# A two-layer trunk: weight casts and a square moved behind evacuations, and gate loads in other buffers

## The chip, the cores and the metric

The kernel runs on one core of a Trainium2 chip. The metric is the device time of one launch in microseconds (us), as a median of several runs. One execution was also taken with the hardware profiler; its trace gives the start and the length of every instruction. The engines are named as in the profile: PE (matmuls), PEld (its weight loads), DVE (vector), ACT (scalar), POOL (GpSimd) and SP, which here only sends DMAs.

## The reference

The input is 1024 tokens of 1024 channels in float32, the output has the same shape. Two layers, each `x + mixer(RMSNorm(x))`, and a last RMSNorm:

```python
def mixer_ab(h, ...):                       # layer 0
    u_s5, g_s5, q, k, v, g_ret = jnp.split(h @ w_in, cuts, axis=-1)
    y_s5 = s5_mixer(u_s5, ...) * jax.nn.silu(g_s5)      # state space, GELU, GLU
    y_ret = retention(q, k, v) * jax.nn.silu(g_ret)    # rotary positions inside
    return jnp.concatenate([y_s5, y_ret], axis=-1) @ w_out

def mixer_conv(h, ...):                     # layer 1
    a, b, g = jnp.split(h @ w_in, 3, axis=-1)
    u = a * jax.nn.sigmoid(b)
    u = causal_depthwise_conv31(u) + conv_b
    u = layernorm_over_channels(u) * ln_g + ln_b
    return (jax.nn.silu(u) * jax.nn.silu(g)) @ w_out
```

## The kernel before

**Layout.** Activations lie with the channels on the 128 partitions, in 8 blocks `nb` of 128 channels, and with the tokens in two halves `h` of 512 on the free axis. Every large product is made with three matmuls of 128x512 for one block of the contraction (`mm3`, L174 to L176): high part by high part, high weights by low activations, low weights by high activations. Operands are rounded to `fp32r`; the low part is what the rounding left out.

**Weights.** `plan` writes down the order in which weight blocks of 512 KB are used. `wnext(name, ahead=2)` hands out the next one and, if that is not yet done, emits the loads of this one and of the two behind it. A load (`wload`) is a DMA on SP into `wf` (L162), a cast on ACT to `wh` (L164), and a subtract on POOL or DVE to `wl` (L165); `wf`, `wh` and `wl` have three buffers each. Weights that are used a second time (`wload_again`) get their low part by DMA from DRAM (L150) in place of the subtract. These are `wl_woc` in the last stage.

**Order.** The program's text is not the order on the engines. A planner with its own estimates of durations orders the instructions of each engine; `with self.at(...)` sets a due time, and `with self.tc.issue_after(x)` keeps what is emitted inside it behind instruction x. In the queue of one engine everything waits behind an instruction that waits. PSUM banks of one kind are handed round: a product that needs a bank waits until the evacuation of its last user is done. `mm` banks are three; in layer 0 there are five `aux` banks beside them.

**Layer 0, values (L1023).** `ret_values_wide` makes the values of the first two pairs of heads, for each half h: four weight blocks `v0_h_j`, each a quarter of the contraction for 512 channels, four banks, one for each 128 tokens, and behind the last block four `nc.scalar.mul` on ACT (L1041) that bring the banks to SBUF scaled by `Rtok`. The next weights in `plan` are k1 and q1. After the values PE turns the keys (`ktp`, L1054), each into an `aux` bank.

**Layer 0 end, layer 1 start.** `w_out(h, nbs)` (L1280 on) makes the output product of layer 0 over 16 blocks, adds the residual on DVE (`x`, L1293), stores it, and adds its square to a running sum (`square_sum`: the square on ACT at L399, the sum on POOL at L404). `ab(h)` makes b and a of layer 1 for each block: weights `cb`, product `mm_b`, tanh on ACT (L1326) for the sigmoid, weights `ca`, product `mm_a`, and `u` on DVE (L1335). In `plan` two blocks of the second half's output product stand ahead of `ab(0)`, the other six behind it. The tanh needs another activation table than what ran before, so an ACT_TABLE_LOAD stands ahead of it.

**Layer 1, convolution.** The convolution runs in pairs of blocks: 26 of 31 taps on DVE (L1393), the first five on ACT and POOL (L1372, L1373), from `u` (tag `u`, five buffers) into a PSUM accumulator. `gates` writes `silu(g)` to DRAM (`gs_d`). `conv_norm(h)` makes the sums over channels with narrow matmuls (`cst` at L435, from `cs` and `cq`, the sums on POOL at L1444 and L1445), spreads mean and deviation over the partitions (`cR`, `cD`), and for each block: norm, SiLU, load of the gate `gl` (L1480), product with it (L1481), and the split into `zh` and `zl` (L1157). In the second half blocks 3, 5 and 7 run on POOL, the others on DVE. `w_out_c` makes the last product `mm_oc` and the final sums (`s2q`, L1507 and L1510).

**Slots in layer 1.** The pool `lp` has rings by tag: `tp` three buffers (partial taps on ACT and POOL, later also the second half's gates), `u` five (the conv's inputs), `ev` three, `ld` two. A load into a ring waits until the last reader of that buffer is done.

Of the kernel before, what the change touches and what calls it, by code (L numbers as in the profile page):

```python
# [11 lines left out]
F32 = mybir.dt.float32  # L12
F32R = mybir.dt.float32r
I32 = mybir.dt.int32
AF = mybir.ActivationFunctionType
# [4 lines left out]
P = 128  # L20
# [3 lines left out]
HALF = 512  # L24
# [27 lines left out]
class Trunk:  # L52
# [59 lines left out]
    def wnext(self, name, ahead=2):  # L112

        assert self.wseq[self.wgot][1] == name, (self.wseq[self.wgot][1], name)
        for i in range(self.wgot, min(self.wgot + ahead + 1, len(self.wseq))):
            if i not in self.wissued:
                self.wissued[i] = self.wload(*self.wseq[i])
        self.wgot += 1
        return self.wissued.pop(self.wgot - 1)

    def wload(self, src, name):

# [900 lines left out]
    def ret_values_wide(self):  # L1023

        nc = self.nc
        res = []
        for h in range(2):
            vt = self.rp.tile([P, 4, HALF], F32, name=f"v_0_{h}", tag="v", bufs=2)
            pss = [self.bank(f"mm_v0_{h}_{b}") for b in range(4)]
            for j in range(4):  # L1030
                wh, wl = (t[:].rearrange("p (k a) n -> p k (a n)", a=4) for t in self.wnext(f"v0_{h}_{j}"))
                for b in range(4):
                    o = slice(b * P, (b + 1) * P)
                    for k in range(2):
                        kb = 2 * j + k
                        xh, xl = self.xs[h][kb]
                        nc.tensor.matmul(pss[b][:], xh[:, o], wh[:, k, :], start=kb == 0, stop=False)
                        nc.tensor.matmul(pss[b][:], xh[:, o], wl[:, k, :], start=False, stop=False)
                        nc.tensor.matmul(pss[b][:], xl[:, o], wh[:, k, :], start=False, stop=kb == KB - 1)
            for b in range(4):  # L1040
                nc.scalar.mul(vt[:, b, :], pss[b][:], self.Rtok[:, 4 * h + b:4 * h + b + 1])  # L1041
            res.append(vt)
        return lambda p, b, hh: res[b // 4][:, b % 4, (2 * p + hh) * P:(2 * p + hh + 1) * P]

    def ret_heads(self, pair, K, Q, qadds, mask, kdec, V, turned):
# [113 lines left out]
    def layer0_back_and_layer1(self, st):  # L1159
        nc, A = self.nc, self.A  # L1160
        v, gp = nc.vector, nc.gpsimd
        lp = self.lp
# [73 lines left out]
        for m in range(2):  # L1236
            pss = [self.bank(f"mm_glu1{2 * m + a}", aux=False) for a in range(2)]
# [11 lines left out]
        for i, x in ((6, t2), (7, t3), (4, t4)):  # L1249
            for m in range(2):  # L1250
                w = wn()
                for a in range(2):
                    n = 2 * m + a
# [9 lines left out]
        for m in range(2):  # L1263
            pss = [self.bank(f"mm_glu5{2 * m + a}", aux=False) for a in range(2)]
            for i, x in ((5, t1), (3, b22)):
                w = wn()
                for a in range(2):
                    n = 2 * m + a
# [12 lines left out]
        accs = {}  # L1281

        def w_out(h, nbs):
            for nb in nbs:
                xt = lp.tile([P, HALF], F32, name=f"xr{nb}_{h}", tag="ld", bufs=2)
                nc.sync.dma_start(xt[:], A["xT"][nb, :, hs(h)])
                ws = self.wnext(f"wos{nb}_{h}")
                wr = self.wnext(f"wor{nb}_{h}")
                ps = self.bank(f"mm_wo{nb}_{h}", aux=False)
                seq = [(ws, ys[h], kb) for kb in range(KB)] + [(wr, yr[h], kb) for kb in range(KB)]  # L1290
                self.gemm_seq(ps[:], seq, self.hold if h and nb == 0 else None)
                t = lp.tile([P, HALF], F32, name=f"x1_{nb}_{h}", tag="ev", bufs=3)
                v.tensor_tensor(t[:], ps[:], xt[:], op=ALU.add)  # L1293
                nc.sync.dma_start(self.x1_d[rows(nb), hs(h)], t[:])
                self.square_sum(lp, t, nb, h, "s1", accs)

        def h1(h):

# [21 lines left out]
        def ab(h):  # L1320
            for nb in range(8):
                wb = self.wnext(f"cb{nb}_{h}")
                pb = self.bank(f"mm_b{nb}_{h}", aux=False)
                self.gemm(pb[:], wb, hx[h])
                sg = lp.tile([P, HALF], F32, name=f"sb{nb}_{h}", tag="ev", bufs=3)
                nc.scalar.activation(sg[:], pb[:], AF.Tanh, scale=0.5)  # L1326
                wa = self.wnext(f"ca{nb}_{h}")
                pa = self.bank(f"mm_a{nb}_{h}", aux=False)
                self.gemm(pa[:], wa, hx[h])
                u = lp.tile([P, PADW + HALF], F32, name=f"u{nb}_{h}", tag="u", bufs=5)  # L1330
                if h == 0:
                    gp.memset(u[:, :PADW], 0.0)
                else:
                    nc.scalar.copy(u[:, :PADW], tail[:, nb, :])
                v.scalar_tensor_tensor(u[:, PADW:], sg[:], 1.0, pa[:], op0=ALU.add, op1=ALU.mult)  # L1335
                if h == 0:
                    nc.scalar.copy(tail[:, nb, :], u[:, HALF:])
                ub[h][nb] = u
# [70 lines left out]
        def csquare(h, nb):  # L1409
            sq = (self.opA.tile([P, HALF], F32, name=f"cvq{nb}_{h}", tag="A1") if h else  # L1410
                  lp.tile([P, HALF], F32, name=f"cvq{nb}_{h}", tag="sq", bufs=1))
            nc.scalar.activation(sq[:], cv[h][nb][:], AF.Square)
            return sq
# [24 lines left out]
        def conv_norm(h):  # L1438
            sm, acc = accs[("cv", h)]
            st = ps_cv.tile([P, HALF], F32, name=f"cst_{h}", tag="cn")  # L1440
            q7 = csquare(h, 7)
            s1, s2 = st[:, 0:256], st[:, 256:512]
            if h == 0:
                gp.tensor_tensor(sm[:], sm[:], cv[h][7][:], op=ALU.add)  # L1444
                gp.tensor_tensor(acc[:], acc[:], q7[:], op=ALU.add)  # L1445
                self.token_sums([(s1, sm[:]), (s2, acc[:])])
            else:
                self.token_sums([(s1, sm[:]), (s2, acc[:]), (s1, cv[h][7][:]), (s2, q7[:])])
            st4 = st[:].rearrange("p (k b x) -> p k b x", k=2, x=64)

            t4 = [lp.tile([P, 4], F32, name=f"cn4_{i}_{h}", tag=f"cn4_{i}", bufs=1) for i in range(4)]
            d4, q4, v4, r4 = (t[:] for t in t4)
            nc.scalar.activation(q4, st4[:, 0, :, 0], AF.Square, scale=1.0 / D)
            nc.scalar.mul(d4, st4[:, 0, :, 0], 1.0 / D)
            v.scalar_tensor_tensor(v4, st4[:, 1, :, 0], 1.0 / D, q4, op0=ALU.mult, op1=ALU.subtract)
            self.rsqrt(r4, v4)
            v.tensor_tensor(d4, d4, r4, op=ALU.mult)
            Rp = ps_cv.tile([P, HALF], F32, name=f"cR_{h}", tag="cn")
            self.spread(Rp[:], r4, lp, f"cR_{h}")
            Dp = ps_cv.tile([P, HALF], F32, name=f"cD_{h}", tag="cn")  # L1460
            self.spread(Dp[:], d4, lp, f"cD_{h}", *(("tp", 3) if h else ("dg", 1)))
            self.norm_mm[h] = self.last_stat, self.last_spread
            R = lp.tile([P, HALF], F32, name=f"RL_{h}", tag="cq", bufs=1)
            dl = lp.tile([P, HALF], F32, name=f"dl_{h}", tag="cs", bufs=1)
            for nb in range(8):
                c = cv[h][nb]

                e1, e = (v, gp) if h == 0 else (gp, gp) if nb in (3, 5, 7) else (v, v)
                z = ps_cv.tile([P, HALF], F32, name=f"zz{nb}_{h}", tag="cv") if e is v else c
                e1.tensor_tensor(z[:], c[:], (R if e1 is gp else Rp)[:], op=ALU.mult)  # L1470
                if nb == 0:
                    nc.scalar.copy(R[:], Rp[:])
                    nc.scalar.copy(dl[:], Dp[:])
                e.tensor_tensor(z[:], z[:], dl[:], op=ALU.subtract)
                nc.scalar.activation(z[:], z[:], AF.Silu, scale=self.vec(V_LNG, nb), bias=self.vec(V_LNB, nb))
                g = lp.tile([P, HALF], F32, name=f"gl{nb}_{h}", **({"tag": "tp", "bufs": 3} if h else
                                                                   {"tag": "ld", "bufs": 2}))

                with self.tc.issue_after(self.low_load["ca1"].ins) if h == 0 and nb < 2 else nullcontext():
                    nc.sync.dma_start(g[:], self.gs_d[rows(nb), hs(h)])  # L1480
                e.tensor_tensor(z[:], g[:], z[:], op=ALU.mult)  # L1481
                pt = (self.opA, "A1") if h and nb == 7 else (opB, f"B{1 - h}")
                a, b = (self.op_tile(*pt, f"z{q}{nb}_{h}") for q in "hl")
                self.split(z[:], a, b, e)
                zs[h][nb] = (a, b)
# [70 lines left out]
        for h in range(2):  # L1556
# [32 lines left out]
            with self.at(430000):  # L1589
                among = {}  # L1590
                last = [w_out_c(h, nb, quarters, among) for nb in (5, 6, 7)]
# [118 lines left out]
```

## Time and profile before

| what | value |
|---|---|
| runs | 1192.55, 1192.85, 1197.18 us; median 1192.85 us |
| profiled execution | 1193.14 us |
| its span, first to last instruction | 1191.4 us |
| granted TensorE clock | 0.999 |
| chain that ended last, share on PE | 91% |
| DMA | 261.47 MB, mean 219 GB/s |
| largest group on DVE (taps, L1393) | 398 instructions, 273.8 us |

In a row of a timeline stand the start and the length in us, the engine, the line, the operation, its output and inputs by the program's names, and in square brackets the idle time of the engine ahead of it with what ended that. In a row of the waits stand the waiting instruction, what it waited for, the total, the count and the longest, in us. A line of several equal instructions ends in x and their number.

### The profile page before, as it was taken

To read this page: it belongs to the slowest core of one execution; us is meant where nothing else is said; L and a number is where in the kernel's file an instruction comes from. 1 tells how busy PE (TensorE), PEld (TensorE's weight loads), DVE (VectorE), ACT (ScalarE), POOL (GpSimd) and SP (SyncE) were. 2 spreads that over 40 slices of the span, in tenths; PEclk is the share of its full clock that TensorE was granted. 3 is DMA by queue.
4 is the path that set the end of the run, shared out by engine and by line. 5 is a ranking of instruction groups with operands and counts; after the bars stand their busy time and mean duration, and the time that the engine had idled before them with its cause. 6 is when DMAs were issued, how large, how long until landed. Compare 5 with 4: busy or idle time off the path is not lost.

```text
span 1191.4 us, 17385 instructions
## 1 busy us (share of the span) xinstructions
PE 1178.9 (99%) x6376; PEld 987.0 (83%) x6376; DVE 847.7 (71%) x1452; ACT 483.8 (41%) x708; POOL 655.4 (55%) x448
## 2 busy tenths in 40 slices
PE   9999999999999999999999999999999999999997
PEld 7788888888888889999878888788888888888877
DVE  7975798777427459576769423599999899999533
ACT  6322233222232232233546323445445675434663
POOL 2059999988145354233563111678553577758643
PEclk9999999999999999999999999999999999999999
DMA  9344355565388676779988986656668654357774
GB/s 352 96 139 136 116 161 181 176 181 172 109 279 289 218 241 185 254 226 360 377 304 293 337 273 212 229 191 212 225 224 282 214 198 145 121 168 242 238 261 161
DMA packets 117638, 261.47 MB, mean 219 GB/s; under 512 B 10672, under 2 KB 42288, under 8 KB 116912
## 3 DMA queue, kind: packets, MB, share of 16 engines
q1 hardware_dynamic: 117552, 260.36, 65.0%
q8 instruction: 50, 0.82, 0.3%
q14 instruction: 36, 0.29, 0.1%
HBM read 181.48 MB, written 74.65 MB: 215 GB/s over the span
## 4 chain that ended last, share of the span: by engine, by line
PE 91%; DVE 3%; DMA 2%; ACT 2%; issue 1%; POOL 1%; SPq 0%; DVEq 0%; POOLq 0%; ACTq 0%
PE mm_g L174 8%; PE mm_g L176 7%; PE mm_g L175 7%; PE mm_wo L174 5%; PE mm_wo L176 5%; PE mm_wo L175 5%; PE mm_b L174 2%; PE mm_b L175 2%; PE mm_b L176 2%; PE mm_a L176 2%; PE mm_a L175 2%; PE mm_a L174 2%; PE mm_oc L175 2%; PE mm_oc L176 2%; PE mm_oc L174 2%; PE mm_u L175 2%
## 5 line engine op out<-in xcount | busy, mean ns | idle before, releaser
L1393 DVE SCALAR_TENSOR_TENSOR cv<-u,convw,cv 128x512 f32<-128x512 f32 x398 | 273.8, 750 | 12.0 <-ACT cv L1379 9.7
L1373 POOL TENSOR_TENSOR tp<-tp,tp 128x512 f32<-128x512 f32 x64 | 83.0, 1297 | 43.9 <-ACT tp L1372 42.6
L174 PE MATMUL mm_g<-xh,wh_g 128*128 128x512 f32 x256 | 101.9, 398 | 0.0
L176 PE MATMUL mm_g<-xh,wl_g 128*128 128x512 f32 x256 | 100.2, 392 | 0.0
L175 PE MATMUL mm_g<-xl,wh_g 128*128 128x512 f32 x256 | 100.2, 391 | 0.0
L1372 ACT ACTIVATE tp<-u,convw 128x512 f32<-128x512 f32 x64 | 45.5, 719 | 35.6 <-POOL tp L1373 35.3
L174 PEld LDWEIGHTS mm_g<-xh,wh_g 128*128 128x128 f32 x256 | 48.1, 188 | 11.7 <-issue 1.2
L404 POOL TENSOR_TENSOR s1q<-s1q,s1q 128x512 f32<-128x512 f32 x12 | 17.8, 1480 | 71.0 <-ACT s1q L399 71.0
L176 PEld LDWEIGHTS mm_g<-xh,wl_g 128*128 128x128 f32 x256 | 48.1, 188 | 10.3
L175 PEld LDWEIGHTS mm_g<-xl,wh_g 128*128 128x128 f32 x256 | 48.1, 188 | 9.9 <-issue 0.4
L175 PE MATMUL mm_oc<-zl,wh_woc 128*128 128x512 f32 (+1 forms) x152 | 54.5, 360 | 0.5 <-POOL zl L1157 0.5
L176 PE MATMUL mm_oc<-zh,wl_woc 128*128 128x512 f32 (+1 forms) x152 | 54.3, 359 | 0.7 <-DMA wl_woc<-lo_woc 0.7
L174 PE MATMUL mm_oc<-zh,wh_woc 128*128 128x512 f32 (+1 forms) x152 | 54.2, 362 | 0.0
L360 DVE TENSOR_TENSOR gt<-mm_g,R 128x512 f32<-128x512 f32 x32 | 21.9, 683 | 43.6 <-PE mm_g L176 43.6
L165 POOL TENSOR_TENSOR wl_v<-wf_v,wh_v 128x1024 fp32r<-128x1024 f32 x12 | 31.2, 2606 | 37.2 <-ACT wh_v L164 37.2
L174 PE MATMUL mm_b<-h1h,wh_cb 128*128 128x512 f32 x128 | 50.0, 390 | 0.9 <-DVE x L1293 0.9
L165 POOL TENSOR_TENSOR wl_glu<-wf_glu,wh_glu 128x1024 fp32r<-128x1024 f32 x14 | 34.8, 2494 | 28.7 <-ACT wh_glu L164 21.6
L174 PE MATMUL mm_g<-h1h,wh_cg 128*128 128x512 f32 x128 | 50.5, 394 | 0.0
L175 PE MATMUL mm_b<-h1l,wh_cb 128*128 128x512 f32 x128 | 50.4, 393 | 0.0
L174 PE MATMUL mm_a<-h1h,wh_ca 128*128 128x512 f32 x128 | 50.3, 393 | 0.0
L174 PE MATMUL mm_wo<-ysh,wh_wos 128*128 128x512 f32 x128 | 50.0, 390 | 0.0
L176 PE MATMUL mm_g<-h1h,wl_cg 128*128 128x512 f32 x128 | 49.9, 390 | 0.0
(490 smaller groups left out, 3665.2 us busy)
## 6 DMA issues: line engine op xcount, KB each, us to landing
wf_g<-w_ab SPq DMA_DIRECT2D x16, 512.0 KB
wf_wos<-w_out SPq DMA_DIRECT2D x16, 512.0 KB
wf_wor<-w_out SPq DMA_DIRECT2D x16, 512.0 KB
wf_cb<-w_c SPq DMA_DIRECT2D x16, 512.0 KB
wf_ca<-w_c SPq DMA_DIRECT2D x16, 512.0 KB
wf_woc<-w_out_c SPq DMA_DIRECT2D x16, 512.0 KB
wf_v<-w_v SPq DMA_DIRECT2D x12, 512.0 KB
wf_cg<-w_c SPq DMA_DIRECT2D x11, 512.0 KB
```

The costliest lines, as they stand in the source:

```text
L165: lo[i].tensor_tensor(wl[:].rearrange(fl)[:, c], wf[:, c], h.bitcast(F32), op=ALU.subtract)
L174: nc.tensor.matmul(ps, wh[:, kb, :], xh, start=start, stop=False, **more)
L175: nc.tensor.matmul(ps, wh[:, kb, :], xl, start=False, stop=False, **more)
L176: self.last_mm = nc.tensor.matmul(ps, wl[:, kb, :], xh, start=False, stop=stop, **more)
L360: nc.vector.tensor_tensor(gt[:, c], ps[:], self.R[:, c], op=ALU.mult)
L404: nc.gpsimd.tensor_tensor(a, a, sq[:], op=ALU.add)
L1372: nc.scalar.mul(sk[:], u[:, k:k + HALF], cw[:, nb, k:k + 1])
L1373: gp.tensor_tensor(s0[:], s0[:], sk[:], op=ALU.add)
L1393: v.scalar_tensor_tensor(dst[:], *tap, accs_[i][:], op0=ALU.mult, op1=ALU.add)
```

## The change

Three places are changed.

1. At the last block of the values `wnext` emits the loads of one weight block ahead instead of two, and the load of the second one ahead (q1: its DMA, cast and subtract) is emitted behind the last of the four evacuations, by a new function `wahead`.
2. The square of `x1` of block 1, second half, is put off (`self.later`), and is emitted, together with the weights that `wnext("ca0_0")` loads ahead, behind the first tanh of layer 1.
3. In `conv_norm` the second half's gates `gl` of blocks 3 to 7 take the tag `u` (the conv inputs' five buffers); those of blocks 0 to 2 stay in `tp`.

```diff
+    def wahead(self, n):
+
+        for i in range(self.wgot, self.wgot + n):
+            if i not in self.wissued:
+                self.wissued[i] = self.wload(*self.wseq[i])
...
             for j in range(4):
-                wh, wl = (t[:].rearrange("p (k a) n -> p k (a n)", a=4) for t in self.wnext(f"v0_{h}_{j}"))
+                wh, wl = (t[:].rearrange("p (k a) n -> p k (a n)", a=4)
+                          for t in self.wnext(f"v0_{h}_{j}", 1 if h and j == 3 else 2))
...
             for b in range(4):
-                nc.scalar.mul(vt[:, b, :], pss[b][:], self.Rtok[:, 4 * h + b:4 * h + b + 1])
+                last = nc.scalar.mul(vt[:, b, :], pss[b][:], self.Rtok[:, 4 * h + b:4 * h + b + 1])
             res.append(vt)
+
+        with self.tc.issue_after(last.ins):
+            self.wahead(2)
...
-                self.square_sum(lp, t, nb, h, "s1", accs)
+                if (nb, h) == (1, 1):
+                    self.later = lambda t=t: self.square_sum(lp, t, 1, 1, "s1", accs)
+                else:
+                    self.square_sum(lp, t, nb, h, "s1", accs)
...
-                nc.scalar.activation(sg[:], pb[:], AF.Tanh, scale=0.5)
-                wa = self.wnext(f"ca{nb}_{h}")
+                tanh = nc.scalar.activation(sg[:], pb[:], AF.Tanh, scale=0.5)
+
+                with self.tc.issue_after(tanh.ins) if h == 0 and nb == 0 else nullcontext():
+                    wa = self.wnext(f"ca{nb}_{h}")
+                    if (nb, h) == (0, 0):
+                        self.later()
...
-                g = lp.tile([P, HALF], F32, name=f"gl{nb}_{h}", **({"tag": "tp", "bufs": 3} if h else
-                                                                   {"tag": "ld", "bufs": 2}))
+                tag, bufs = ("ld", 2) if h == 0 else ("tp", 3) if nb < 3 else ("u", 5)
+                g = lp.tile([P, HALF], F32, name=f"gl{nb}_{h}", tag=tag, bufs=bufs)
```

## Prediction

> **What bounds the kernel now.** I read the page's busy times first, then the waits of TensorE, then the timeline of each engine around the places that the change touches, and last the two listings of the instruction order side by side.
>
> ```profile
> PE 1178.9 (99%) x6376; PEld 987.0 (83%) x6376; DVE 847.7 (71%) x1452; ACT 483.8 (41%) x708; POOL 655.4 (55%) x448
> ```
>
> TensorE (PE) is busy for 1178.9 of the 1191.4 us of the span. No edit here adds or removes a matmul, so all that can be won is in the 12.5 us in which PE stands still, and all that can be lost is new standing still. What ends those pauses is in the waits of PE:
>
> ```profile
> PE mm_b L174 <- DVE x L1293: 0.9, 1, 0.9
> PE ktp L1054 <- ACT v L1041: 0.8, 1, 0.8
> PE mm_glu L174 <- DVE gu L1260: 0.8, 1, 0.8
> PE mm_oc L176 <- DMA wl_woc<-lo_woc: 0.7, 2, 0.4
> PE rf_ps L435 <- ACT s2q L1507: 0.6, 1, 0.6
> PE mm_oc L175 <- POOL zl L1157: 0.5, 1, 0.5
> ```
>
> The columns are total us, times, longest us. Three places of this list are those that the change works on: the first row (start of layer 1's input products), the second (behind the values), and the fourth with the sixth (the last output product). The third row, `gu`, is not touched, but lies downstream of the second and comes back among the rivals.
>
> **Part 1: q's cast behind the values.** ACT and PE around 397 us:
>
> ```profile
> 396.32 1.05 ACT L164 CAST wh_q<-wf_q 128x1024 fp32r<-128x1024 f32 x1 [3.25 <-PE mm_v L1038]
> 397.27 1.26 ACT L1041 ACTIVATE v<-mm_v,Rtok 128x512 f32<-128x512 f32 x2
> ```
> ```profile
> 396.74 0.48 PE L174 MATMUL mm_k<-xh,wh_k 128*128 128x512 f32 x1
> 398.00 0.33 PE L1054 MATMUL ktp<-ident,krot 128*128 128x128 f32 x1 [0.79 <-ACT v L1041]
> ```
>
> PE goes from the values to k's product and the turned keys (`ktp`). The second `ktp` needs a bank that a `v` evacuation empties. ACT's order has the cast of `wh_q` ahead of the four `v`, and that cast cannot start before PE has let go of an older weight buffer (mm_v at L1038). So the cast holds the evacuations from 396.32 to 397.3. The `ktp` starts 1.26 us after the matmul ahead of it, where the pace is 0.23 us; 1.03 us is lost. In the new order the four `v` stand ahead of `wh_q`. The first needs only its own bank, which is complete 18 matmuls (4.1 us) before the last value matmul, and ACT stood idle for 3.25 us before the cast; so that bank is empty by 394 and the wait goes, 1.03 us.
>
> What is moved: one cast on ACT (1.05 us) and the subtract on GpSimd that makes `wl_q`. The DMA of `wf_q` keeps its place on SP (only the table `kdec` changes places with it). Behind the new place, `wh_q` starts after the last `v`, about 397.2 instead of 396.32. Its user, q's product, stands behind k's product of 48 matmuls, 48 x 0.23 = 11 us, so the 0.9 us of delay has cover; without that cover it would cost 0.9.
>
> Is the 1.03 us kept to the end? The next wait of PE is 200 us later:
>
> ```profile
> 595.60 2.87 DVE L1157 TENSOR_TENSOR y22l<-y22f,y22h 128x512 fp32r<-128x512 f32 x1
> 598.40 0.67 DVE L1260 TENSOR_TENSOR gu<-gu,mm_glu 128x512 f32<-128x512 f32 x1
> 599.00 0.68 DVE L1157 TENSOR_TENSOR y22l<-y22f,y22h 128x512 fp32r<-128x512 f32 x1
> ```
> ```profile
> 595.10 2.83 POOL L165 TENSOR_TENSOR wl_glu<-wf_glu,wh_glu 128x1024 fp32r<-128x1024 f32 x1
> ```
>
> PE waits 0.8 us for `gu`. DVE reaches `gu` at 598.40, behind a `y22l` that took 2.87 us beside GpSimd's weight subtract, where the one after it took 0.68 us alone. If those two come earlier with everything else, the gain passes; if they are held by transfers, PE arrives earlier and waits for the same `gu`. Ends 0 and 1.03; nothing in the rows decides between them, so I take the middle, **0.5**. The Trainium skill ("SBUF — State Buffer", "Who interferes with whom") says that a DVE instruction with two inputs in SBUF contends with a GpSimd instruction that reads SBUF, and that the one that holds the shared ports keeps them for its whole instruction. The 2.87 beside the 0.68 us agrees; by that rule `gu` follows GpSimd's clock and not PE's, the term would be 0, and the sum below 1.9 instead of 2.4.
>
> **Part 2: layer 1's first tanh.** ACT and PE around 759 us:
>
> ```profile
> 754.04 1.05 ACT L164 CAST wh_cb<-wf_cb 128x1024 fp32r<-128x1024 f32 x1 [6.10 <-PE mm_b L175]
> 758.80 1.05 ACT L164 CAST wh_ca<-wf_ca 128x1024 fp32r<-128x1024 f32 x1 [3.71 <-PE mm_a L175]
> 759.75 1.04 ACT L164 CAST wh_cb<-wf_cb 128x1024 fp32r<-128x1024 f32 x1
> 760.70 0.63 ACT L399 ACTIVATE s1q<-x 128x512 f32<-128x512 f32 x1
> 761.35 1.28 ACT L1326 ACT_TABLE_LOAD   x1
> 762.64 0.60 ACT L1326 ACTIVATE sb<-mm_b 128x512 f32<-128x512 f32 x1
> ```
> ```profile
> 759.01 0.39 PE L176 MATMUL mm_wo<-yr1h,wl_wor 128*128 128x512 f32 x1
> 760.27 0.47 PE L174 MATMUL mm_b<-h1h,wh_cb 128*128 128x512 f32 x1 [0.87 <-DVE x L1293]
> ```
>
> The first tanh's input is complete at about 754 (the cast at 754.04 is released by that product's matmuls), yet the tanh runs at 762.64, because two casts that wait for PE and the square of the last `x` stand ahead of it. Its bank is therefore not free when PE comes to the second `mm_b`, and PE takes the bank that `x` empties at 760.1: 1.26 us between starts instead of 0.23, 1.03 lost. In the new order ACT does `wh_cb`, table load, tanh, then `wh_ca`, `wh_cb`, square. The tanh would end at 754.04 + 1.05 + 1.28 + 0.60 = 757.0, and in the listing the second `mm_b` now waits for ACT's tanh alone. PE reaches it at 759.01 + 0.23 = 759.24, 2.2 us after that. The wait goes: **1.0**; if something still held the tanh for more than 2.2 us, part of it would stay.
>
> What is moved, with its DMA: `ca`'s load on SP keeps its order against the neighbours; its cast waits for PE's `mm_a` until 758.80 anyway and by then the tanh is over, so it costs nothing. The square (0.63) keeps its place behind the two casts; without the table load ahead of them it ends at about the same 761.3, and the running sum on GpSimd behind it is wanted only by the norm of the second half, tens of us later. The first conv input `u` comes some 3 us earlier on DVE, since it waited for the tanh. DVE goes on to the taps in a changed order; that is Part 4.
>
> **Part 3: gates of the last product.** PE, SP and GpSimd in the last stage:
>
> ```profile
> 1131.82 0.39 PE L174 MATMUL mm_oc<-zh,wh_woc 128*128 128x512 f32 x1
> ...
> 1137.96 0.50 PE L176 MATMUL mm_oc<-zh,wl_woc 128*128 128x512 f32 x1 [0.39 <-DMA wl_woc<-lo_woc]
> ...
> 1140.55 0.50 PE L175 MATMUL mm_oc<-zl,wh_woc 128*128 128x512 f32 x1 [0.48 <-POOL zl L1157]
> ```
> ```profile
> 1126.41 0.99 SPq L1480 DMA_DIRECT2D gl<-gs_d  x2
> 1127.49 0.38 SPq L150 DMA_DIRECT2D wl_woc<-lo_woc  x1
> ...
> 1132.08 0.32 SPq L1480 DMA_DIRECT2D gl<-gs_d  x1
> 1132.49 0.38 SPq L150 DMA_DIRECT2D wl_woc<-lo_woc  x1
> ```
> ```profile
> 1136.73 1.29 POOL L1481 TENSOR_TENSOR co<-gl,co 128x512 f32<-128x512 f32 x1 [2.71 <-DMA gl<-gs_d]
> 1137.97 1.29 POOL L1510 TENSOR_TENSOR s2q<-s2q,s2q 128x512 f32<-128x512 f32 x1
> 1139.22 2.52 POOL L1157 TENSOR_TENSOR zl<-co,zh 128x512 fp32r<-128x512 f32 x2
> ```
>
> From 1131.82 to 1140.55 the program has 30 matmuls; at 0.227 us they take 6.81 of the 8.73 us, so 1.92 us is lost: to two loads of `wl_woc`, to `zl`, and to slower restarts behind each. The five gates `gl` of the blocks 3 to 7 get slots that the taps free far earlier, so SP can send them between 1033 and 1106 us and not in the queue here. Two things follow. SP's `wl_woc` of block 1 goes about 0.9 us earlier (without the pair of `gl` ahead of it), that of block 2 about 0.4. The first wait (0.7 - 0.39 = 0.3) goes. The second (0.39) only shrinks: its load was used 1137.96 - 1132.49 = 5.4 us after it was sent, and is sent 0.4 earlier. And GpSimd's multiply at 1136.73, which waited 2.71 us for a `gl`, runs ahead; its three multiplies come first, then `s2q`, then `zl`, so that `zl` of block 3 ends about 1139.1 where the first of the pair ended at 1140.5. Lower end: the first wait with its restart, 0.4. Upper end 1.92. PE is then at block 3 by 1138.6, so about 0.5 of the wait for `zl` and some of the second load may stay; I take **1.1**. New on SP: a `gl` now waits in its queue for DVE's last tap at five places. The rows queued behind each are sent later than the tap's end in the old trace, so nothing is held; if a conv came late, the load behind the `gl` would be held as long.
>
> **Part 4: what is reshuffled.** Between 760 and 965 the taps of DVE, GpSimd and ACT stand in another order, and the sums of the first half's norm stand about 2 us earlier in PE's order.
>
> ```profile
> 942.26 1.28 POOL L1445 TENSOR_TENSOR cq<-cq,cvq 128x512 f32<-128x512 f32 x1
> ```
> ```profile
> 945.20 0.39 PE L175 MATMUL mm_b<-h1l,wh_cb 128*128 128x512 f32 x1
> ```
>
> The sums over `cq` now come behind the matmul of 945.20 and four narrow ones (0.45 us): 945.9, less the 1.5 us that PE is ahead by then, 944.4. GpSimd has `cq` at 943.54. That leaves 0.85 us; bounds for a new wait are 0 and 1.5 (nothing moved up on GpSimd and one more add ahead of it). With 0.85 in hand it is nearer to the first: **-0.2**.
>
> **Sum.** 0.5 + 1.0 + 1.1 - 0.2 = 2.4 us off the profiled execution of 1193.14: 1190.7. The median of the runs (1192.85) is 0.29 below that execution, so 1190.4. A measurement can tell about 0.5%, 6.0 us, from no change.
>
> **Rivals.**
>
> *The gain of 397 us dies at 598.* `gu` comes when GpSimd's third subtract and the loads let it. For it: GpSimd's subtract and DVE's `y22l` end within 0.5 us of each other, and the wait is already there. Against: nothing says that these do not start earlier too. 1.9 in place of 2.4: 1190.95. Chance 0.17.
>
> *The gates were hidden.* The last stage's transfers take as long as before, because the bytes are the same and `wl_woc` is what is late; only the 0.4 comes, and 397 is lost too: 1.0 + 0.4 - 0.2 = 1.2, so 1191.65. Chance 0.12.
>
> *Slower: the first half's conv comes late.* The place is the pair of sums near 944 us.
>
> ```profile
> 759.00:910.00 151.00, 150.13 (x670) 124.08 (x668) 139.59 (x208) 75.49 (x111) 103.24 (x70) 1.00 0.68 231
> ```
>
> In this stage (columns: length, busy PE, PEld, DVE, ACT, POOL, clock, DMA share, GB/s) DVE is busy 139.59 of 151 us. A delay of the taps there has only 11 us of slack to be made good, and PE now asks for the sums 2 us sooner. Each us by which `cq` ends later than 944.4 is a us of PE. It gets slower than before once that is 2.6 us; at 5 us it gives 1193.14 - 2.6 + 5 - 0.29 = 1195.2, and beyond 0.5% only from 8.6. Against it: `u` comes 3 us earlier, which pulls the taps forward. Chance 0.06, of which 0.03 is beyond 0.5%.
>
> *More than 0.5% faster.* That is 6 us; the three places hold 1.03 + 1.03 + 1.92 = 4.0 together. Chance 0.03.
>
> **Numbers.** The forecast has 0.62. Its own best end is a gain of 4.0: 1188.8, and 0.4 of scatter between executions gives the low end 1188.4. Its weak ends lie in the second and third cases, up to 1191.65; the range goes on to 1194.0 for the lighter half of the slower case. Faster by over 0.5% 0.03, slower by over 0.5% 0.03, within it 0.94.
>
> **What would show it.** In the profile after, PE's waits on `v` and on `x` at L1293 are gone; the first tanh runs near 756.4 to 757; the five `gl` leave SP between 1033 and 1106 us; `zl` ends by 1139.2 less the gain until then, and the two waits for `wl_woc` add up to under 0.4. Part 1 is half wrong if the wait for `gu` has grown from 0.8 towards 1.8. The prediction is wrong if PE's list has a new row of over 1 us, above all one for `cs` or `cq`, or if the three places stay.

## The result

The changed kernel takes 1189.27 us (median of 13 runs, 1187.82 to 1191.94) against 1193.34 us of the kernel before, run beside it (13 runs, 1190.82 to 1197.18). The medians lie 4.1 us apart. The ratio, which goes by all the runs and not by the two medians, is 0.9970, with a 95% interval of 0.9958 to 0.9982: 3.6 us faster, between 2.1 and 5.0. The forecast was 1190.4 us in 1188.4 to 1194.0.

The profiled execution, 1191.94 us, is the longest of the 13; its span of 1190.1 us is only 1.3 us shorter than before's. So the profile shows less of a gain than the times do. The page's first row and the list of PE's waits, of the changed kernel (lines there are 6 to 17 higher than before):

```profile
PE 1178.1 (99%) x6376; PEld 987.2 (83%) x6376; DVE 847.0 (71%) x1452; ACT 483.8 (41%) x708; POOL 654.4 (55%) x448
```
```profile
PE rt L1155 <- DVE mv L1142: 1.2, 1, 1.2
PE idle L272 <- DVE mhalf L217: 1.1, 1, 1.1
PE mm_glu L180 <- DVE gu L1270: 0.8, 1, 0.8
PE mm_glu L180 <- ACT sg L1239: 0.6, 1, 0.6
PE rf_ps L441 <- ACT s2q L1524: 0.6, 1, 0.6
PE mm_glu L182 <- POOL wl_glu L171: 0.3, 1, 0.3
PE ss L441 <- DVE ssum L267: 0.3, 1, 0.3
PE mm_oc L181 <- POOL zl L1167: 0.3, 1, 0.3
```

The waits for `v`, for `x` and for `wl_woc` are gone, that for `zl` has shrunk from 0.5 to 0.3. New are `rt` (1.2) and `sg` (0.6), both between 570 and 577 us, in a part of layer 0 that the change does not touch. No row names `cs` or `cq`.

Three landmarks on PE divide the run: the first `mm_wo`, the first `mm_oc`, and the first `rf_wait` just ahead of the last sums. From PE's timeline, before and after:

```profile
635.03 0.39 PE L174 MATMUL mm_wo<-ysh,wh_wos 128*128 128x512 f32 x1
...
1082.85 0.39 PE L174 MATMUL mm_oc<-zh,wh_woc 128*128 128x512 f32 x1
...
1183.11 1.11 PE L469 MATMUL rf_wait<-ones 128*128 128x128 f32 x8
```
```profile
636.36 0.39 PE L180 MATMUL mm_wo<-ysh,wh_wos 128*128 128x512 f32 x1
...
1083.08 0.39 PE L180 MATMUL mm_oc<-zh,wh_woc 128*128 128x512 f32 x1
...
1181.79 1.11 PE L475 MATMUL rf_wait<-ones 128*128 128x128 f32 x8
```

The changed kernel reaches `mm_wo` 1.33 us later than before did, needs 446.72 instead of 447.82 us from there to `mm_oc` (part 2 lies in this section), and 98.71 instead of 100.26 us from there to `rf_wait` (part 3). Parts 2 and 3 gave 1.10 and 1.55 us; the section with part 1 lost 1.33 in this execution.

The first tanh, on ACT:

```profile
755.37 1.05 ACT L170 CAST wh_cb<-wf_cb 128x1024 fp32r<-128x1024 f32 x1 [6.10 <-PE mm_b L181]
756.44 1.28 ACT L1339 ACT_TABLE_LOAD   x1
757.74 0.60 ACT L1339 ACTIVATE sb<-mm_b 128x512 f32<-128x512 f32 x1
```

It runs at once behind the cast, 2.2 us ahead of its use, and the second `mm_b` follows the last `mm_wo` in step (760.34, then 760.57). The five gates left SP at 1033.42, 1056.44, 1072.46, 1093.99 and 1106.46, as named. In the last stage, on SP, POOL and PE:

```profile
1126.81 0.32 SPq L156 DMA_DIRECT2D wl_woc<-lo_woc  x1
...
1132.25 0.32 SPq L156 DMA_DIRECT2D wl_woc<-lo_woc  x1
```
```profile
1132.89 3.83 POOL L1498 TENSOR_TENSOR co<-gl,co 128x512 f32<-128x512 f32 x3
1136.67 1.32 POOL L1527 TENSOR_TENSOR s2q<-s2q,s2q 128x512 f32<-128x512 f32 x1
1137.92 3.80 POOL L1167 TENSOR_TENSOR zl<-co,zh 128x512 fp32r<-128x512 f32 x3
```
```profile
1136.59 0.39 PE L182 MATMUL mm_oc<-zh,wl_woc 128*128 128x512 f32 x1
...
1138.17 0.84 PE L180 MATMUL mm_oc<-zh,wh_woc 128*128 128x512 f32 x3
1139.28 0.50 PE L181 MATMUL mm_oc<-zl,wh_woc 128*128 128x512 f32 x1 [0.27 <-POOL zl L1167]
```

No gate stands on SP between the two `wl_woc` any more; POOL makes the three products in one go from 1132.89 instead of waiting 2.71 us for the second. The first `zl` ends near 1139.2, which is the one short wait that is left. The matmul at 1136.59 is the first that uses the second `wl_woc`, and it does not wait.

The trace also holds the times at which a load's semaphore was counted up; the last of a load's 16 counts is its landing. The second `wl_woc` landed at 1137.92 in before, 5.43 us after it was sent, and at 1136.16 in the changed kernel, 3.91 us after. In the kernels of the experiments below it is 5.36 and 5.55 us without part 3 (part 1 alone, part 2 alone) and 3.78 to 4.20 with it (part 3 alone, parts 2 and 3, the whole change again). Sent at 1132.25 but with the old 5.43 us it would have landed at 1137.68, 1.1 us behind its use: it is the shorter time under way with the gates gone from the queue, and not the earlier sending, that took this wait away.

### The profile page after: what moved, and what is told of

Same layout as the page of the kernel before. It is cut to its first block, busy times and chain, and to the rows that moved or that the text cites. A ratio compares the mean times of both kernels' runs of the same rounds, so it can differ in the third digit from the quotient of the medians.

```text
span 1190.1 us, 17385 instructions
## 1 busy us (share of the span) xinstructions
PE 1178.1 (99%) x6376; PEld 987.2 (83%) x6376; DVE 847.0 (71%) x1452; ACT 483.8 (41%) x708; POOL 654.4 (55%) x448
## 4 chain that ended last, share of the span: by engine, by line
PE 47%; DMA 3%; DVE 2%; issue 1%; POOL 1%; ACT 1%; SPq 0%; DVEq 0%; POOLq 0%; ACTq 0%
PE mm_wo L180 5%; PE mm_wo L181 5%; PE mm_wo L182 5%; PE mm_g L180 2%; PE mm_b L182 2%; PE mm_g L182 2%; PE mm_b L181 2%; PE mm_g L181 2%; PE mm_b L180 2%; PE mm_a L180 2%; PE mm_a L181 2%; PE mm_a L182 2%; PE mm_oc L181 2%; PE mm_oc L182 2%; PE mm_oc L180 2%
## 5 line engine op out<-in xcount | busy, mean ns | idle before, releaser
L182 PE MATMUL mm_a<-h1h,wl_ca 128*128 128x512 f32 x128 | 50.2, 392 | 0.0
L182 PE MATMUL mm_b<-h1h,wl_cb 128*128 128x512 f32 x128 | 49.9, 390 | 0.0
```

The costliest lines, as they stand in the source:

```text
L182: self.last_mm = nc.tensor.matmul(ps, wl[:, kb, :], xh, start=False, stop=stop, **more)
```

## The experiments

Two theories on part 1: its gain is carried to the end, or it is swallowed between 550 and 600 us by what the DMA queue delivers. First the parts alone, with the others undone.

**Part 1 alone** (only the two edits in `ret_values_wide` and `wahead`).

> Part 1 alone (q's cast behind the values). Theory A (carried): the wait of ktp for v, 0.8 us with its restart 1.03, goes, and PE stays about 1.0 us ahead to the end: about 1.0 us less than before. Theory B (swallowed): the wait goes as well, PE is 1.0 ahead until about 560 us, and is then held by what the DMA queue delivers between 555 and 600 us (wf_glu, then the loads behind gu): the waits of PE between 560 and 601 us grow by about 1.0 us in sum and the time is that of before, within 0.3.

**Part 2 alone** (only `self.later` and the tanh's block).

> Part 2 alone (first tanh ahead of two casts and a square). Both theories: the wait of mm_b for x at 759 us (0.9, with restart 1.03) goes and nothing ahead of 759 changes: 1.0 us less than before. A rival, that the reshuffled taps cost at the norm of the first half, would show a new wait of PE for cs or cq near 944 us, and no gain.

**Part 3 alone** (only the tags of `gl`).

> Part 3 alone (five gates of the second half into the conv inputs' buffers). By the forecast 1.1 us less than before; by the profile after, where the two waits for wl_woc are gone and the wait for zl is 0.3, about 1.5 less. If the earlier loads of gl hold up SP between 1033 and 1106 us, a wait for a weight appears in that stretch and takes some of it back.

**Parts 2 and 3.** Against the changed kernel:

```diff
-                          for t in self.wnext(f"v0_{h}_{j}", 1 if h and j == 3 else 2))
+                          for t in self.wnext(f"v0_{h}_{j}"))
...
-        with self.tc.issue_after(last.ins):
-            self.wahead(2)
```

> The change without part 1. Theory A (carried): 1.0 us more than the whole change, about 2.5 less than before. Theory B (swallowed): the same time as the whole change within 0.3 us; PE keeps its 0.8 us wait for v at 397 us, and its waits between 560 and 601 us are smaller than in the whole change by about that.

Measured on one chip, against 1193.54 us of before (32 runs):

| kernel | median us | ratio to before, 95% |
|---|---|---|
| part 1 alone | 1193.39 | 1.0003 (0.9993 to 1.0014) |
| part 2 alone | 1191.93 | 0.9984 (0.9972 to 0.9997) |
| part 3 alone | 1191.88 | 0.9988 (0.9977 to 0.9999) |
| parts 2 and 3 | 1190.07 | 0.9973 (0.9959 to 0.9987) |

Parts 2 and 3 together have the gain of the whole change (0.9973 against 0.9970), though their interval has room for 1 us more or less. Part 1 alone has none that can be told; a gain of 1.0 us would be a ratio of 0.9992, just outside its interval. In the times that looks like the swallowed theory. The profiles tell another story. The one of part 1 alone has no wait of PE between 397 and 632 us at all, and its execution took 1190.74 us, the shortest of its 12. And of the kernels without part 1, those with part 2 alone and with parts 2 and 3 have no wait for `v` either. ACT at 395 us, of part 3 alone (with its wait of PE), of part 2 alone, and of part 1 alone:

```profile
396.49 1.05 ACT L170 CAST wh_q<-wf_q 128x1024 fp32r<-128x1024 f32 x1 [3.25 <-PE mm_v L1044]
397.44 2.42 ACT L1047 ACTIVATE v<-mm_v,Rtok 128x512 f32<-128x512 f32 x4
```
```profile
PE ktp L1060 <- ACT v L1047: 0.8, 1, 0.8
```
```profile
394.92 1.05 ACT L170 CAST wh_q<-wf_q 128x1024 fp32r<-128x1024 f32 x1 [3.29 <-DMA wf_q<-w_ab]
395.87 2.42 ACT L1047 ACTIVATE v<-mm_v,Rtok 128x512 f32<-128x512 f32 x4
```
```profile
392.88 0.68 ACT L1048 ACTIVATE v<-mm_v,Rtok 128x512 f32<-128x512 f32 x1
...
397.18 1.04 ACT L170 CAST wh_q<-wf_q 128x1024 fp32r<-128x1024 f32 x1
```

Without part 1 the evacuations follow the cast of `wh_q`, and that follows the landing of `wf_q`. The profile names `mm_v` as what ended the wait in before and in part 3 alone, but the semaphore of the load says otherwise: its last count comes at 396.22 in before and at 396.39 in part 3 alone, and 0.10 us later the cast begins, as it does in the three profiles that name the load. In five profiles with before's order on ACT (before, the relief below, and the three kernels without part 1 here) the cast began 0.07 us (before) and 0.01 us (part 3 alone) ahead of the first `ktp`, with a wait of 0.8 each; and 1.28, 2.60 and 3.12 us ahead of it in the other three, with none. Two of five: part 1 takes away about 1 us in some executions and nothing in the others, an estimate of 0.4 us on the average, from these five profiles alone. The DMA share from 380 to 396 us is 0.97 to 1.08 in windows of 5 or 6 us, with the wait and without; what makes the load land sooner or later was not found.

What becomes of that 1 us can be followed for 150 us. From the first `ktp` after the values to the first `mm_glu` PE takes 151.48 us in before and 151.53 in part 3 alone, the two with the wait, and 150.52 in part 1 alone, 150.47 in part 2 alone and in parts 2 and 3, 150.47 and 150.74 in the two profiles of the whole change. So where the wait is, it costs 1.0 us, and this is still missing when the glu starts. From the first `mm_glu` to the first `mm_wo` it then takes 85.78 us in part 1 alone, 86.92 and 89.50 in the whole change, and 86.24 to 87.18 in before and the three kernels without part 1. This scatter hides 1 us; whether it is swallowed there stays open.

**Relief of the queue at 550 us.** The second question was whether the stretch up to `mm_wo`, in which executions differ most, is set by the DMA queue. The relief sends two groups of loads later.

```diff
-                        t3 = load_sum("yt3", 1, 1, 1)
+                        with self.tc.issue_after(self.wf_load["glu4"].ins):
+                            t3 = load_sum("yt3", 1, 1, 1)
...
-                nc.sync.dma_start(xt[:], A["xT"][nb, :, hs(h)])
+                with self.tc.issue_after(self.wf_load["glu13"].ins) if h == 0 and nb < 2 else nullcontext():
+                    nc.sync.dma_start(xt[:], A["xT"][nb, :, hs(h)])
```

(`wf_load` holds the DMA of each weight.) On before:

> Before, with two groups of loads taken out of the way of the weights in the stretch 550 to 600 us: the second operand sum yt3 (8 loads of 256 KB) is sent behind the fifth weight of the glu, and the first two residual blocks xr (2 loads of 256 KB) behind its last weight. Nothing else is moved. If what PE waits for between 560 and 601 us is set by the DMA queue (swallowed), the stretch from the first mm_glu to the first mm_wo gets shorter than the 87.2 us of before, towards the 85.8 us that it took in the profile of part 1 alone where it had no waits, and the time falls by 0.5 to 1.5 us. If the DMA queue has no part in it, nothing changes.

With part 1:

> The relief with part 1. Swallowed by the DMA queue: with the queue relieved the 1.0 us of part 1 is now kept, 1.0 us less than the relief alone. If part 1 gives nothing for another reason (its wait is replaced by another one that the queue has no part in): the same as the relief alone.

With all three parts:

> The relief with all three parts. Swallowed by the DMA queue: 1.0 to 2.0 us less than the whole change, 5 to 6 us less than before, and no wait of PE over 0.5 us between 560 and 601. Otherwise: the time of the whole change.

And the whole change beside them:

> The whole change once more, on the chip of the three runs beside it, for a second profile and for their comparison: 3 to 4 us less than before. If the 2.2 us of waits for mv and sg at 570 to 576 us in its first profile belong to the change, they are there again; if they belong to that one execution, the stretch from the first mm_glu to the first mm_wo takes less than the 89.5 us of then.

Against 1193.89 us of before (35 runs): the relief 1194.26 (1.0010, 1.0001 to 1.0018), with part 1 1193.18 (1.0004, 0.9992 to 1.0015), with all parts 1191.57 (0.9987, 0.9975 to 0.9999), the whole change 1190.26 (0.9970, 0.9959 to 0.9981). The relief alone made things worse by 1.2 us (0.1 to 2.1) where a gain was expected. With all parts it lies 2.0 us above the whole change by the ratios, and with part 1 0.7 us below the relief alone; in both the intervals overlap. What it holds back was not found in its single profiles. In the one on before the stretch from the first `mm_glu` to the first `mm_wo` took 85.98 us, short as expected, but the late load below took 85.86 without any relief. It does not tell the theories of part 1 apart. The whole change came out at 0.9970 again, and its second profile has neither `rt` nor `sg`: these belong to that first execution. There ACT stood in front of a late weight of the glu, with the `rs` of the norm behind it in its queue, which PE's `rt` needs; in the second profile the same cast began at 563.34 and `rs` at 565.69, 1.4 us earlier:

```profile
564.78 1.05 ACT L170 CAST wh_glu<-wf_glu 128x1024 fp32r<-128x1024 f32 x1 [3.21 <-DMA wf_glu<-w_glu]
565.85 1.28 ACT L450 ACT_TABLE_LOAD   x1
567.14 0.30 ACT L450 ACTIVATE rs<-mv,epst 128x4 f32<-128x4 f32 x1
```

**A late load of q's weights,** without and with part 1:

```diff
-            nc.sync.dma_start(wf[:, c], src.rearrange(fl)[:, c])
+            for _ in range(2 if name == "q1" else 1):
+                nc.sync.dma_start(wf[:, c], src.rearrange(fl)[:, c])
```

> Before, with the load of q1's weights sent twice, one behind the other into the same buffer, so that it is complete some 3 to 4 us later than the 393.9 to 396.5 us at which its cast began in the profiles so far. If the wait for v at 397 us is a wait for that load (ACT holds the evacuations behind q1's cast), it is now there for certain and grows to 2.5 to 4.5 us, and the time rises by 2 to 4 us over before. If the wait has another cause, it stays at 0 to 0.8 us and the time with it.

> The same late load together with part 1. If part 1 does nothing but take the evacuations out of that load's reach, PE has no wait for v, the late weights are still in time for q's product some 10 us later, and the time is that of before within 0.5 us: 2 to 4 us less than the late load without part 1. If the late load comes through at q's product instead, a wait for wh_q or wl_q of 1 us or more appears after 405 us.

Against 1194.24 us of before (34 runs): 1192.62 (0.9986, 0.9974 to 0.9998) and 1193.30 (0.9987, 0.9975 to 0.9999). The expected 2 to 4 us of loss did not come. ACT without part 1:

```profile
392.93 0.69 ACT L1042 ACTIVATE v<-mm_v,Rtok 128x512 f32<-128x512 f32 x1 [0.56 <-PE mm_v L1040]
394.29 0.69 ACT L1042 ACTIVATE v<-mm_v,Rtok 128x512 f32<-128x512 f32 x1 [0.67 <-PE mm_v L1040]
400.76 1.05 ACT L165 CAST wh_q<-wf_q 128x1024 fp32r<-128x1024 f32 x1 [5.78 <-DMA wf_q<-w_ab]
401.71 0.68 ACT L1042 ACTIVATE v<-mm_v,Rtok 128x512 f32<-128x512 f32 x1
```

Two of the four evacuations stand ahead of the cast here: the planner, which orders by its own estimates, had moved them on its own. The cast then begins at 400.8, 3.9 us behind the first `ktp`, and PE has no wait for `v`: the two banks that are free by then are enough here. So a larger wait could not be made, but the run shows the same thing from the other side: with the first `v` ahead of the cast, a landing of `wf_q` at 400.4 to 400.7 does not reach PE, with part 1 or without. Why both are some 1.6 us faster than before by their ratios, while part 1 alone was not, stays open.

**The fourth `gu` ahead of the splits,** on the whole change:

```diff
-                        v.tensor_tensor((u2 if i == 6 else u3)[n][:], u2[n][:], ps[:], op=ALU.add)
+                        gu = v.tensor_tensor((u2 if i == 6 else u3)[n][:], u2[n][:], ps[:], op=ALU.add)
...
-                t1, b22 = load_sum("yt1", 0, 1, 0), load_split(B(1, 1), "y22", 1, False)
+                t1, b22 = load_sum("yt1", 0, 1, 0), load_split(B(1, 1), "y22", 1, False, gu)
```

> The whole change, and in the glu DVE makes the fourth gu ahead of the splits y22l instead of behind two of them; this is the gu for which PE waited 0.5 to 1.0 us near 598 us in most profiles. If that wait is DVE's order (y22l slow beside GpSimd), it goes and the time falls by about 0.8 us below the whole change, to about 0.9963 of before. If PE is held there by the loads anyway, it waits for the next thing (wl_glu or a second operand) and the time is that of the whole change.

1189.39 us, 0.9965 of before (0.9953 to 0.9976). DVE in the whole change's second profile, with PE's wait, then in this kernel, and in part 1 alone:

```profile
594.68 3.91 DVE L1167 TENSOR_TENSOR y22l<-y22f,y22h 128x512 fp32r<-128x512 f32 x2
598.52 0.68 DVE L1270 TENSOR_TENSOR gu<-gu,mm_glu 128x512 f32<-128x512 f32 x1
```
```profile
599.25 0.50 PE L180 MATMUL mm_glu<-yt3h,wh_glu 128*128 128x512 f32 x1 [1.00 <-DVE gu L1270]
```
```profile
594.79 0.67 DVE L1270 TENSOR_TENSOR gu<-gu,mm_glu 128x512 f32<-128x512 f32 x1
595.38 4.07 DVE L1167 TENSOR_TENSOR y22l<-y22f,y22h 128x512 fp32r<-128x512 f32 x3
```
```profile
595.08 1.71 DVE L1167 TENSOR_TENSOR y22l<-y22f,y22h 128x512 fp32r<-128x512 f32 x2
596.71 0.67 DVE L1270 TENSOR_TENSOR gu<-gu,mm_glu 128x512 f32<-128x512 f32 x1
```

`gu` runs 3.7 us earlier, ends at 595.46, and PE uses its bank at 598.35 without a wait; it was 1.0 us in that second profile. So with this order the wait has 2.9 us to spare. It can also go without the edit: in part 1 alone the two splits take 1.71 instead of 3.91 us, and PE has no wait there either. From the first `mm_glu` to the first `mm_wo` PE takes 86.13 us in this profile, 86.92 in the whole change's second one and 85.78 in part 1 alone, so the sections do not show a gain. By its ratio it is the fastest kernel of all, but the 0.0005 that it lies below the whole change is inside the intervals.

**Fewer loads,** on the whole change:

```diff
-                    t2, t3 = (load_sum("yt2", 0, 0, 1), None) if m == 0 else (t2, load_sum("yt3", 1, 1, 1))
+                    t2, t3 = (load_sum("yt2", 0, 0, 1), None) if m == 0 else (t2, t2)
```

> The whole change without the 8 loads of yt3 (2 MB between 552 and 562 us); the product that uses it reads yt2 in its place, so this leaves out part of the glu's operands. If the scatter from run to run and the waits between 560 and 601 us come from the full DMA queue, the waits between 560 and 601 shrink to under 0.5 us, the stretch from the first mm_glu to the first mm_wo comes to about 86 us, and the time falls by 0.5 to 1.5 us below the whole change. If not, it is the time of the whole change.

This kernel leaves out `yt3`, and so part of the glu's operands. 1196.99 us, 1.0024 of before (1.0015 to 1.0033): slower. The glu's weights do land earlier (the cast that stood at 564.78 in the whole change begins at 560.99), but the planner's new order puts a `y22l` into the gap. DVE, and the wait of PE that follows:

```profile
563.07 2.04 DVE L1167 TENSOR_TENSOR y22l<-y22f,y22h 128x512 fp32r<-128x512 f32 x1 [5.63 <-ACT y22h L1165]
565.04 1.27 DVE L1106 TENSOR_TENSOR sc<-sp,retmask 128x512 f32<-128x512 f32 x2
```
```profile
565.77 2.08 PE L1127 MATMUL ro<-S,qrot 64*128 64x128 f32 x14 [3.69 <-DVE sc L1106]
```

`y22l` waits 5.6 us at the head of DVE's queue, with retention's `sc` behind it and PE behind that. The expectation on the queue is not tested by this; what it shows is a wait of 3.69 us that came through an order.

**All profiles side by side.** Each column is the time from the landmark before it, in us:

| profile | to first `mm_wo` | to first `mm_oc` | to `rf_wait` |
|---|---|---|---|
| before | 635.03 | 447.82 | 100.26 |
| part 1 alone | 632.70 | 447.83 | 100.16 |
| part 2 alone | 633.51 | 446.94 | 100.37 |
| part 3 alone | 634.27 | 447.85 | 98.73 |
| parts 2 and 3 | 634.68 | 446.72 | 98.77 |
| whole change | 636.36 | 446.72 | 98.71 |
| whole change, again | 634.58 | 446.72 | 98.75 |
| late load | 633.15 | 447.83 | 100.11 |
| late load, part 1 | 632.73 | 447.84 | 100.33 |
| `gu` first | 634.38 | 446.72 | 98.71 |
| relief | 634.34 | 447.82 | 100.14 |
| relief, part 1 | 637.89 | 447.82 | 100.33 |
| relief, all parts | 634.76 | 446.71 | 98.73 |
| fewer loads | 639.94 | 446.72 | 98.73 |

The middle column falls by 1.1 with part 2 (0.9 when alone) and else repeats within 0.03; the last falls by 1.3 to 1.7 with part 3 and else repeats within 0.26. The first column moves by 5.2 us even without the fewer loads, and by 1.8 between two profiles of the same kernel.

## Why the prediction was right

- **What bounds it** held: the two sections that repeat fall by little else than the waits that went, with the slower restarts behind them. These came to 1.03 of the 1.10 us in the middle section. In the last one the 30 matmuls up to the wait for `zl` took 7.23 us (1132.05 to 1139.28) instead of 8.73: 1.50 of the 1.55.
- **Part 2** was forecast at 1.0 and measured at 1.1. The tanh ran at 757.74, in an execution that was 1.33 us behind; in before's time that is 756.4, the near end of the 756.4 to 757 named.
- **Part 3** was forecast at 1.1 and measured at 1.55. The mis-sized term is the second `wl_woc`: the prediction kept the 5.4 us from sending to use, and so some of the wait. The load landed 3.91 us after it was sent and PE did not wait for it. This also answers the rival of the hidden gates: with them gone the same bytes of `wl_woc` were 1.5 us less under way. What was said of `zl` held to 0.1 us: end near 1139.1, part of a 0.5 wait left (0.27).
- **Part 1** was forecast at 0.5, between 0 and 1.03. Measured alone it lies between a loss of 1.7 and a gain of 0.8 us, so the term is within the interval, but the reasoning behind it was wrong at one step, the reading of a row: the idle time ahead of the cast was put down to PE's `mm_v`, as the profile has it, and so taken for a fixed part of the program. The cast waits for the landing of `wf_q`, and PE's wait is there in two of five profiles. That an average of 0.4 us comes near the forecast 0.5 is luck: the 0.5 was the middle between a gain kept and a gain lost, and not a share of executions. Where the wait is, its 1.0 us is kept up to the first `mm_glu`; whether it reaches the end was not settled.
- **The rival at 598 us**: the wait for `gu` stayed 0.8 and 1.0 in the two profiles of the whole change, and was absent in that of part 1 alone. The Trainium skill ("SBUF — State Buffer", "Who interferes with whom") says that a DVE instruction with two inputs in SBUF contends with a GpSimd instruction that reads SBUF. By that rule the prediction's rival had the term at 0. The time of part 1 alone has room for 0, and the traces agree on the contention: in the nine profiles in which the second `y22l` begins beside GpSimd's third `wl_glu` (before, the three reliefs, the three kernels without part 1, both of the whole change) it takes 2.87 to 2.88 us, and PE waits 0.5 to 1.0 us for `gu` in seven of them and 0.1 and 0.2 in two; in part 1 alone and the two late loads that subtract is over, `y22l` takes 0.68 us and the wait is under 0.2. With `gu` moved ahead a `y22l` still took 2.87 us and PE did not wait. So in these profiles a wait of 0.5 us or more needs both, the contention and the order. That `gu` would hold part 1's gain in every execution is not shown.
- **Part 4** was forecast at -0.2 and cost nothing: POOL ended `cq` at 941.27 + 1.30 = 942.57, a us earlier than before, and PE's first `cst` ran at 944.74 without a wait.
- The forecast sum of 2.4 lies inside the measured 2.1 to 5.0. The two sections that repeat give 2.65; of the rest nothing can be told from the scatter of the first section. The 0.4 us of scatter in the low end of the range is small beside the 4.1 us between single executions of the changed kernel. The slower rival did not come.

## What to carry to other kernels

A wait in one profile may be a matter of that execution: before an edit is priced at it, look whether what it waits for is the landing of a load, and take a second profile. Where the total scatters by more than the effect, start times of the same instruction at landmarks give a part's worth to 0.1 to 0.3 us, if the sections between them repeat; parts 2 and 3 could be told in this way, part 1 could not be to its end. And where a planner sets the order, every experiment changes more than its edit: read the order first; the late load and the fewer loads both went another way because of it.

## What was not expected of the hardware

The same program differs by 4.1 us among 13 executions of the changed kernel (1187.82 to 1191.94, granted clock 0.998 to 0.999), by 7.4 us among 34 of before (1191.44 to 1198.87, 0.997 to 0.999), and by 1.8 us up to the first `mm_wo`, while the section of 446.72 us behind it is the same in both profiles of the changed kernel. A load of 512 KB, sent into a queue with a DMA share of 0.97 to 1.08, landed anywhere from 3.2 to 0.1 us ahead of PE's first `ktp` in five profiles, and the wait of 0.8 us was there in the two in which it landed last. The same DVE instruction `y22l` took 0.68 us alone and 2.88 us beside a GpSimd subtract. A load of 512 KB, the second `wl_woc`, was 5.4 to 5.6 us under way with three gates of 256 KB sent from 0.4 us ahead of it to 1.6 us behind it, and 3.8 to 4.2 us without them.
